# A float32 decoder trunk: the second MLP product as seven half-sized products, with the residual stream kept as [token, feature]

## The chip, the cores and the metric

The kernel runs on one core of a Trainium2 chip. The metric is the device time of one execution in microseconds (us), as the median of several runs. The engines are named as in the profile: PE (TensorE: matmuls and transposes, with its loads of the stationary operand as PEld), DVE (VectorE), ACT (ScalarE), POOL (GpSimd), and SP (SyncE, which issues DMAs).

## The reference

A trunk of two layers over 512 tokens of 1024 features in float32: layer 0 mixes tokens by stick-breaking attention, layer 1 by a gated linear recurrence (HGRN2), and an MLP follows each. Before each part stands an RMSNorm, behind it an addition to the residual stream.

```python
def squared_relu_mlp(h, w1, w2):          # w1: 1024 x 4096, w2: 4096 x 1024
    a = jax.nn.relu(h @ w1)
    return (a * a) @ w2

for layer in range(2):
    h = rmsnorm(x, norm_gains[layer, 0])
    x = x + (stick_breaking_mixer(h, ...) if layer == 0 else hgrn2_mixer(h, ...))
    h = rmsnorm(x, norm_gains[layer, 1])
    x = x + squared_relu_mlp(h, mlp_w1[layer], mlp_w2[layer])
```

## The kernel before

Every large product is computed in three passes: each operand is split into a rounded part `hi` (type fp32r) and the rest `lo`, and `hi*hi + hi*lo + lo*hi` is summed in PSUM. A matmul takes a stationary block of 128x128 and a moving operand of up to 512 columns, so one output tile over 1024 inputs takes 8 x 3 = 24 matmuls.

The residual stream is kept transposed: eight tiles `xT` of [128 features, 512 tokens] (L347). In `gemm_w` (L314) weights are stationary and 512 tokens move past them. A weight slab is 1024 rows by 256 columns. `Weights.prepare` (L274) loads it in two halves (`wr`, three buffers), ACT casts each half to `wh` (L265), DVE subtracts to get `wl` (L266); `wh` and `wl` have two buffers each. `Weights.next` hands out one slab and prepares the following, so a slab is prepared while its predecessor is used, and cannot be before the one ahead of that is done with.

`mlp` (L656) runs four rounds over blocks of 1024 hidden features. A round takes four slabs of w1 and makes eight hidden tiles: DVE evacuates PSUM with relu and the norm's factor into `u` (L674), ACT squares it (`a`, L678), DVE splits it into `hh` and `hl` (L680, L681). Then four slabs of w2 make eight output tiles, which DVE adds to `xT` (L697). PSUM tiles of the tag `mm` have two buffers, `z` two, `tr` three.

A norm's inputs are split from `xT` tile by tile as they are completed (`Norm.add`, L366); the sums of squares over features are made by ACT squares, DVE additions and small matmuls (`sums`, L376). `finish` (L393) computes r = 1/rms and spreads it over the partitions as `R` while `two` (L649) already multiplies the first slab. At the end `store` (L980) transposes each output tile back on PE, ACT copies it to SBUF and SP sends it out.

PE's order is the order of the program, with side tasks (`Line`, L120) placed by waits in `LAG` counted in estimated PE time. The order on the other engines is made by the scheduler of the framework when the kernel is built, by the program's order and its own estimates; on the chip every engine then takes its queue strictly in that order.

Of the kernel before, what the change touches and what calls it, by code (L numbers as in the profile page):

```python
# [30 lines left out]
def level_columns(H, skip):  # L31
# [8 lines left out]
    "st": 4.96,  # L40
    "bc": 4.0,
# [8 lines left out]
    "o": 2.04,  # L50
# [8 lines left out]
def trunk(  # L59
# [209 lines left out]

    class Weights:  # L270
# [3 lines left out]
        def prepare(self):  # L274
            if self.plan:
                hi, lo, load, split = slab_halves(self.plan.pop(0))
                for a in range(2):
                    split(a, load(a))
                self.ready.append((hi, lo))
# [67 lines left out]
    xT = [cp.tile([P, S], F32, name=f"xT{k}") for k in range(KT)]  # L347

    class Norm:


        def __init__(self, layer, j):
            self.layer, self.j = layer, j
            self.acts, self.acc = [], None

        def split(self, k, src=None):
            src = xT[k] if src is None else src
# [6 lines left out]
            self.acts.append((hi, lo))  # L364

        def add(self, k):  # L366
            self.split(k)
            if self.acc is None:
                self.acc = sb("bc", name="acc")
                nc.scalar.activation(out=self.acc, in_=xT[k], func=AF.Square)  # L370
            else:
                sq = sb("sq", name="sq")
                nc.scalar.activation(out=sq, in_=xT[k], func=AF.Square)
                nc.vector.tensor_add(self.acc, self.acc, sq)

        def sums(self):  # L376
            p = ps("tr", name="ps_st")
            for t in range(TT):
                mm(p[:, t : t + 1], blk(self.acc, t), ones[:, 0:1], True, True)
            return p[:, 0:TT]  # L380
# [12 lines left out]
        def finish(self):  # L393

            yield LAG["st"]
            sums = self.sums()
            _, self.r = self.stats(sums)
# [20 lines left out]
    def attention(norm):  # L418
# [23 lines left out]
        ss = sb("ss", (P, 4, TT), name="ssx")  # L442
        wsl, xin, raws = start["w"], start["x"], start["raws"]
        first = [ps("mm"), ps("mm"), ps("z"), ps("z")]
        with tc.manual_schedule(
            engines={mybir.EngineType.Activation, mybir.EngineType.DVE}
        ):
            for c in range(5):
                if c < 4:
                    turned = []  # L450
                    for j in range(2):
                        k = 2 * c + j
                        p = ps("tr", name="ps_x")
                        for t in range(TT):
                            tr(blk(p, t), xin[c][:, t, j * P : (j + 1) * P])
                        norm.split(k, p)
                        turned.append(p)
# [630 lines left out]
```

## Time and profile before

| | |
|---|---|
| median of 3 runs | 1311.36 us (1311.09 to 1312.01) |
| the profiled execution | 1314.0 us, span 1312.3 us |
| granted PE clock, mean | 0.997 |
| PE / DVE / ACT / POOL busy | 98% / 61% / 34% / 6% |
| attention and its projection | 0 to about 309 us |
| first MLP | about 309 to 659 us |
| recurrence and its projection | about 659 to 955 us |
| second MLP | about 955 us to the end |
| weights and inputs read | 107.4 MB, mean 83 GB/s over the span with the output |

In rows of groups of instructions the columns are: line, engine, operation, output<-inputs by the program's names, shape, count; then busy us and mean ns of one; then the idle time of the engine just before them and what ended it. A row of the timeline gives start, length, engine, line, operation, operands and count, and in brackets the idle time before it. In a row of one tile's instructions three numbers stand for the shortest, the median and the longest, in ns. Matmuls are pipelined: a matmul that is listed with 389 ns is followed by the next after less than that.

### The profile page before, as it was taken

To read this page: it belongs to the slowest core of one execution; us is meant where nothing else is said; L and a number is where in the kernel's file an instruction comes from. 1 tells how busy PE (TensorE), PEld (TensorE's weight loads), DVE (VectorE), ACT (ScalarE), POOL (GpSimd) and SP (SyncE) were. 2 spreads that over 40 slices of the span, in tenths; PEclk is the share of its full clock that TensorE was granted. 3 is DMA by queue.
4 is the path that set the end of the run, shared out by engine and by line. 5 is a ranking of instruction groups with operands and counts; after the bars stand their busy time and mean duration, and the time that the engine had idled before them with its cause. 6 is when DMAs were issued, how large, how long until landed. Compare 5 with 4: busy or idle time off the path is not lost.

```text
span 1312.3 us, 17619 instructions
## 1 busy us (share of the span) xinstructions
PE 1288.4 (98%) x6993; PEld 1103.6 (84%) x6993; DVE 798.1 (61%) x1534; ACT 446.0 (34%) x756; POOL 79.7 (6%) x139
## 2 busy tenths in 40 slices
PE   7999999999999999999999999999999999999998
PEld 7989898778888888888888888888888888888887
DVE  5787688768534435345578888787774354453441
ACT  5555454544212222123433333342432122221221
POOL 0100000000000000000013222222000000000000
PEclk9999999999999999999999999999999999999999
DMA  6312121113333333333321312221323333333331
GB/s 181 107 33 65 33 65 65 45 52 94 97 98 97 97 96 98 96 96 97 97 85 47 94 58 72 65 65 65 96 86 103 95 99 98 95 100 95 99 96 48
DMA packets 110658, 110.64 MB, mean 84 GB/s; under 512 B 3849, under 2 KB 106417, under 8 KB 110577
## 3 DMA queue, kind: packets, MB, share of 16 engines
q1 hardware_dynamic: 110496, 109.22, 26.9%
q8 instruction: 55, 0.90, 0.3%
q0 software_dynamic: 80, 0.31, 0.1%
q14 instruction: 27, 0.21, 0.1%
HBM read 107.41 MB, written 2.10 MB: 83 GB/s over the span
## 4 chain that ended last, share of the span: by engine, by line
PE 83%; DVE 10%; issue 2%; POOL 2%; ACT 1%; SPq 1%; DMA 0%; DVEq 0%; POOLq 0%; ACTq 0%
PE ps_mm L153 70%; PE po L153 3%; PE ps_z L153 3%; POOL tot L814 2%; DVE sc L847 2%; DVE wl L266 2%; PE ps_s L153 2%; PE pa L157 1%; PE z L153 1%; DVE qr L828 1%; PE po_h L153 1%; DVE sn L593 1%; DVE X L865 1%; DVE X L869 1%; DVE ql L565 1%
## 5 line engine op out<-in xcount | busy, mean ns | idle before, releaser
L265 ACT CAST wh<-wr 128x1024 fp32r<-128x1024 f32 x198 | 199.9, 1052 | 391.2 <-PE ps_mm L153 355.5
L266 DVE TENSOR_TENSOR wl<-wr,wh 128x1024 fp32r<-128x1024 f32 x198 | 237.4, 1229 | 17.5 <-ACT wh L265 16.8
L153 PE MATMUL ps_mm<-xh,wh 128*128 128x512 f32 x592 | 232.1, 392 | 0.0
L153 PE MATMUL ps_mm<-xh,wl 128*128 128x512 f32 x592 | 230.5, 389 | 0.0
L153 PE MATMUL ps_mm<-xl,wh 128*128 128x512 f32 x592 | 230.4, 389 | 0.0
L153 PE MATMUL ps_mm<-hh,wh 128*128 128x512 f32 (+1 forms) x520 | 201.3, 387 | 0.0
L153 PE MATMUL ps_mm<-hh,wl 128*128 128x512 f32 (+1 forms) x520 | 200.7, 386 | 0.0
L153 PE MATMUL ps_mm<-hl,wh 128*128 128x512 f32 (+1 forms) x520 | 200.6, 386 | 0.0
L153 PE MATMUL ps_mm<-wh,xh 128*128 128x256 f32 x592 | 173.3, 293 | 0.0
L153 PE MATMUL ps_mm<-wl,xh 128*128 128x256 f32 x592 | 167.7, 283 | 3.8 <-DVE wl L461 3.3
L153 PE MATMUL ps_mm<-wh,xl 128*128 128x256 f32 x592 | 167.5, 283 | 0.0
L697 DVE TENSOR_TENSOR xT<-xT,ps_mm 128x512 f32<-128x512 f32 x63 | 43.3, 687 | 203.5 <-PE ps_mm L153 203.5
L153 PEld LDWEIGHTS ps_mm<-xh,wl 128*128 128x128 f32 x592 | 111.1, 188 | 23.1
L153 PEld LDWEIGHTS ps_mm<-xl,wh 128*128 128x128 f32 x592 | 111.2, 188 | 22.6
L153 PEld LDWEIGHTS ps_mm<-xh,wh 128*128 128x128 f32 x592 | 111.2, 188 | 22.5
L153 PEld LDWEIGHTS ps_mm<-wl,xh 128*128 128x128 f32 x592 | 113.4, 192 | 4.8 <-DVE wl L461 3.5
L153 PEld LDWEIGHTS ps_mm<-wh,xh 128*128 128x128 f32 x592 | 113.2, 191 | 4.2 <-issue 3.6
L674 DVE SCALAR_TENSOR_TENSOR u<-ps_mm,R 128x512 f32<-128x512 f32 x60 | 41.5, 691 | 123.1 <-PE ps_mm L153 123.1
L153 PEld LDWEIGHTS ps_mm<-hl,wh 128*128 128x128 f32 x520 | 97.7, 188 | 19.6
L153 PEld LDWEIGHTS ps_mm<-hh,wl 128*128 128x128 f32 x520 | 97.7, 188 | 19.6
L153 PEld LDWEIGHTS ps_mm<-hh,wh 128*128 128x128 f32 x520 | 97.7, 188 | 19.5
L153 PEld LDWEIGHTS ps_mm<-wh,xl 128*128 128x128 f32 x592 | 113.4, 192 | 0.0
(213 smaller groups left out, 1651.6 us busy)
## 6 DMA issues: line engine op xcount, KB each, us to landing
wr<-in_mlp_w_dram SPq DMA_DIRECT2D x128, 512.0 KB, 3.8
wr<-in_hg_w_in_dram SPq DMA_DIRECT2D x32, 512.0 KB, 3.8
wr<-in_sb_w_qkv_dram SPq DMA_DIRECT2D x22, 512.0 KB, 3.6
wr<-in_sb_w_o_dram SPq DMA_DIRECT2D x8, 512.0 KB, 4.3
wr<-in_hg_w_o_dram SPq DMA_DIRECT2D x8, 512.0 KB, 3.6
xin<-in_x_dram SPq DMA_DIRECT2D x8, 256.0 KB, 5.4
out_dram<-o SPq DMA_DIRECT2D x7, 256.0 KB, 2.3
wr<-in_sb_w_qkv_dram SPq DMA_DIRECT2D x4, 256.0 KB, 5.4
```

The costliest lines, as they stand in the source:

```text
L153: nc.tensor.matmul(o, lhsT=lhsT, rhs=rhs, start=start, stop=stop, **kw)
L157: nc.tensor.transpose(o, in_, ident)
L265: nc.scalar.copy(hi[:, c, :], raw)
L266: nc.vector.tensor_tensor(out=lo[:, c, :], in0=raw, in1=f(hi[:, c, :]), op=ALU.subtract)
L565: nc.vector.tensor_tensor(out=ql[i][own, :], in0=pq[own, :], in1=f(qh[i][own, :]), op=ALU.subtract)
L593: nc.vector.tensor_tensor_scan(out=rev, data0=rev, data1=later[:, S - W :][:, ::-1], initial=1.0, op0=ALU.mult, op1=ALU.max,)
L674: nc.vector.scalar_tensor_tensor(out=u, in0=p, scalar=0.0, in1=norm.R, op0=ALU.max, op1=ALU.mult)
L697: nc.vector.tensor_add(xT[m], xT[m], p)
L814: nc.gpsimd.tensor_tensor(out=tots[H][:, :, None], in0=t0, in1=t1, op=ALU.mult)
L828: nc.vector.tensor_tensor(out=q1, in0=q1, in1=t0.to_broadcast([P, S // (2 * H), H]), op=ALU.mult)
L847: nc.vector.copy_predicated(out=o, mask=mask.rearrange("p (g w) -> p g w", g=g)[:, None].to_broadcast([P, 2, g, w]), data=data.rearrange(" ...
L865: nc.vector.tensor_tensor(out=o, in0=qv[:, :, :, part * H : part * H + w], in1=tv[:, :, :, part - 1, None].to_broadcast([P, TT, g, w]), op ...
```

## The change

The second product of a round is h (512 tokens x 1024) times a 1024x1024 block of w2. Both are cut into quarters: A11, A21 (tokens 0-255 and 256-511 of hidden tiles 0-3), A12, A22 (of tiles 4-7), and B11, B12, B21, B22. Seven products of quarter size replace eight (Winograd's form of Strassen's identity). They use A11, A12, A22 and four sums of quarters (`s1` to `s4`), and B11, B21, B22 and four differences. The results go back into the residual stream by additions, some through a tile `U`.

- *Stationary and moving.* The output is now [token, feature]: activation blocks are stationary, 512 columns of weights move (`chain`). The residual stream is two tiles `xt[h]` of [128, 4 token tiles, 512 features]. The output projections of the mixers use the same form.
- *Activations* (`Seven.take`). Tiles 0-3: ACT squares and casts, DVE subtracts for A11, POOL makes the difference A11-A21. Tiles 4-7: ACT squares and casts three times, DVE makes three `lo` of 512 columns (`a2l`, `s31l`, `s42l`) and two subtractions of 256 columns (`a`), POOL one addition of 256.
- *Weights* (`quarters`, `seven`). The four quarters of a w2 block are loaded whole during the w1 slabs into tiles of other tags (B, X5, R4). Seven slabs of 512 rows by 512 columns are split from them; the `lo` of two are made on POOL, of five on DVE. Of the four differences, POOL makes three (called T1, T3 and the last) and DVE one (T2), each in two subtractions of 1024 columns.
- *Norms.* Squares are summed by ACT with an accumulator (`squares`). Both halves of the features are turned by PE transposes (`turning`) and split from PSUM; `two` multiplies the half that is ready first. The initial copies into `xT` go, and the output is sent straight from `xt`.

```diff
+        def slab(src, eng=nc.vector):
...
+            for a in range(2):
+                c = slice(2 * a, 2 * a + 2)
+                nc.scalar.copy(hi[:, c, :], src[a])
+                eng.tensor_tensor(out=lo[:, c, :], in0=src[a], in1=f(hi[:, c, :]), op=ALU.subtract)
+            return hi, lo
+        def b11():
+            got = slab(b[0, 0])
+            minus(nc.gpsimd, b[0, 0], b[0, 1], b[0, 0])
+            minus(nc.gpsimd, b[0, 1], b[1, 1], b[0, 1])
+            return got
+        def t1():
+            got = slab(b[0, 0])
+            minus(nc.vector, b[0, 0], b[1, 1], b[0, 0])
+            return got
+        def t2():
+            got = slab(b[0, 0])
+            minus(nc.gpsimd, b[1, 0], b[1, 0], b[0, 0])
+            return got
+        slabs = [
+            b11, lambda: slab(b[1, 0], nc.gpsimd), t1, t2, lambda: slab(b[1, 1], nc.gpsimd),
+            lambda: slab(b[0, 1]), lambda: slab(b[1, 0]),
+        ]
...
-            got += [full(mlp_w1[layer], 0, q * D + c * SLAB) for c in range(4)]
-            got += [full(mlp_w2[layer], q * D, c * SLAB) for c in range(4)]
+            loads, slabs = seven(mlp_w2[layer], q * D)
+            for c in range(4):
+                got += [full(mlp_w1[layer], 0, q * D + c * SLAB), loads[c]]
+            got += slabs
...
+        def turning(self, h, lag):
+            yield lag
+            for k in range(4 * h, 4 * h + 4):
+                p = ps("tr", name="ps_x")
+                for t in range(TT):
+                    tr(blk(p, t), blk(xt[h][:, t, :], k - 4 * h))
+                self.split(k, p)
+                yield LAG["x2"]
...
+    def chain(o, wsl, acts):
+        hi, lo = wsl
+        n = len(acts)
+        for k, (ah, al) in enumerate(acts):
+            mm(o, ah, hi[:, k, :], k == 0, False)
+            mm(o, ah, lo[:, k, :], False, False)
+            mm(o, al, hi[:, k, :], False, k == n - 1)
+            yield
...
+            k -= 4
+            a, raw = sb("sn", name="a"), self.raw[k]
+            self.raw.append(a)
+            nc.scalar.activation(out=a, in_=u, func=AF.Square)
+            nc.gpsimd.tensor_tensor(out=raw[:, B], in0=raw[:, B], in1=a[:, B], op=ALU.add)
+            self.a2.append(self.two_parts(a, "Q", "a2"))
+            nc.vector.tensor_tensor(out=a[:, B], in0=a[:, B], in1=raw[:, A], op=ALU.subtract)
+            nc.vector.tensor_tensor(out=a[:, A], in0=a[:, A], in1=a[:, B], op=ALU.subtract)
+            self.s31.append(self.two_parts(raw, "qT", "s31"))
+            self.s42.append(self.two_parts(a, "Q" if k < 2 else "qT", "s42"))
...
+        steps = [
+            ("a11", p1), ("a12", p2), ("s1", p5), ("s2", p6), ("s4", p3), ("s3", p7), ("a22", p4),
+        ]
+        for n, (name, then) in enumerate(steps):
+            wsl = weights.next()
+            for t in range(2):
+                p = ps("z" if n % 2 else "mm", name="ps_mm")
+                yield from chain(p, wsl, A.part(name, t))
+                then(t, p)
```

In `LAG`, "st" (4.96) and "o" (2.04) go, "x" 1.6, "x7" 3.0 and "x2" 0.5 come, and "bc" goes from 4.0 to 8.5.

The change also reorders what stands in the queues. On DVE, before, around the last two hidden tiles of the first MLP's second round (numbers are those of the program's tiles; `u_4291` and `u_4324` are the tiles 6 and 7):

```order
L674 SCALAR_TENSOR_TENSOR u_4291<-ps_mm_4266,R_3534 128x512 [waits PE_49]
L680 CAST hh_4295<-a_4293 128x512 [waits Activation_49]
L681 TENSOR_TENSOR hl_4296<-a_4293,hh_4295 128x512 [waits DVE_49]
L674 SCALAR_TENSOR_TENSOR u_4324<-ps_mm_4299,R_3534 128x512 [waits PE_49]
L266 TENSOR_TENSOR wl_4333<-wr_4334,wh_4332 128x1024 [waits DMAHW1_49,Activation_49]
L266 TENSOR_TENSOR wl_4333<-wr_4338,wh_4332 128x1024 [waits DMAHW2_49,Activation_49]
L680 CAST hh_4328<-a_4326 128x512 [waits Activation_49]
L681 TENSOR_TENSOR hl_4329<-a_4326,hh_4328 128x512 [waits DVE_49]
L697 TENSOR_TENSOR xT0_99<-xT0_99,ps_mm_4342 128x512 [waits PE_49]
```

Now, in the same place, from tile 5's `a2l` to tile 7's evacuation (`a_4340` belongs to tile 5, `u_4396` and `a_4398` to tile 6, `u_4440` to tile 7):

```order
L780 TENSOR_TENSOR a2l_4344<-a_4340,a2h_4343 128x512 [waits Activation_49]
L772 TENSOR_TENSOR a_4340<-a_4340,raw_a_4169 128x256 [waits DVE_49,Pool_49]
L780 TENSOR_TENSOR s31l_4350<-raw_a_4169,s31h_4349 128x512 [waits Activation_49]
L773 TENSOR_TENSOR a_4340<-a_4340 128x256 [waits DVE_49]
L854 SCALAR_TENSOR_TENSOR u_4396<-ps_mm_4371,R_3520 128x512 [waits PE_49]
L780 TENSOR_TENSOR s42l_4354<-a_4340,s42h_4353 128x512 [waits Activation_49]
L780 TENSOR_TENSOR a2l_4402<-a_4398,a2h_4401 128x512 [waits Activation_49]
L780 TENSOR_TENSOR s31l_4408<-raw_a_4216,s31h_4407 128x512 [waits Activation_49]
L772 TENSOR_TENSOR a_4398<-a_4398,raw_a_4216 128x256 [waits DVE_49]
L773 TENSOR_TENSOR a_4398<-a_4398 128x256 [waits DVE_49]
L780 TENSOR_TENSOR s42l_4412<-a_4398,s42h_4411 128x512 [waits Activation_49]
L854 SCALAR_TENSOR_TENSOR u_4440<-ps_mm_4415,R_3520 128x512 [waits PE_49]
```

Between two evacuations of PSUM there stood two instructions on a tile; now there stand six, some of which wait for POOL (by themselves, or by ACT's cast of what POOL made).

On POOL, before, nothing stood between the attention's clearing of `ql` and the recurrence:

```order
L559 MEMSET ql_2767 64x512
L559 MEMSET ql_2768 64x512
L559 MEMSET ql_2847 64x512
L559 MEMSET ql_2848 64x512
L814 TENSOR_TENSOR tot_5914<-fr_5885 128x256
L814 TENSOR_TENSOR tot_5914<-tot_5914 128x128
```

Now, in the same round as above, with `raw_4095`/`raw_4097` the two halves of B11, `raw_4175`/`raw_4177` of B12, `raw_4255`/`raw_4257` of B22, `raw_4357`/`raw_4359` of B21, and the 256-column additions those of tiles 4 to 7:

```order
L770 TENSOR_TENSOR raw_a_4136<-raw_a_4136,a_4296 128x256 [waits Activation_49,Pool_49]
L293 TENSOR_TENSOR raw_4095<-raw_4175,raw_4095 128x1024 [waits DMAHW4_49,DMAHW2_49,DVE_49]
L770 TENSOR_TENSOR raw_a_4169<-raw_a_4169,a_4340 128x256 [waits Activation_49,Pool_49]
L293 TENSOR_TENSOR raw_4175<-raw_4255,raw_4175 128x1024 [waits DMAHW6_49,Pool_49]
L293 TENSOR_TENSOR raw_4097<-raw_4177,raw_4097 128x1024 [waits DMAHW5_49,DMAHW3_49,DVE_49]
L293 TENSOR_TENSOR raw_4177<-raw_4257,raw_4177 128x1024 [waits DMAHW7_49,Pool_49]
L770 TENSOR_TENSOR raw_a_4216<-raw_a_4216,a_4398 128x256 [waits Activation_49]
L305 TENSOR_TENSOR wl_4460<-raw_4357,wh_4459 128x1024 [waits DMAHW0_49,PE_49,Activation_49]
L305 TENSOR_TENSOR wl_4460<-raw_4359,wh_4459 128x1024 [waits DMAHW1_49,Activation_49]
L770 TENSOR_TENSOR raw_a_4249<-raw_a_4249,a_4442 128x256 [waits Activation_49]
L293 TENSOR_TENSOR raw_4357<-raw_4357,raw_4095 128x1024 [waits DVE_49,Pool_49]
L293 TENSOR_TENSOR raw_4359<-raw_4359,raw_4097 128x1024 [waits DVE_49,Pool_49]
```

The four subtractions for T1 and T3 stand ahead of the addition for tile 6, and the two `lo` of the second slab ahead of that for tile 7.

More of the change, by code (lines that the diff above doesn't have):

```diff
@@ L49 @@
     "m": 8.82,
-    "o": 2.04,
     "head": [
@@ L353, in __init__, with split @@
             self.layer, self.j = layer, j
-            self.acts, self.acc = [], None
-        def split(self, k, src=None):
-            src = xT[k] if src is None else src
+            self.acts, self.ss, self.turned = [None] * KT, None, []
+        def split(self, k, src):
             g = gain(self.layer, self.j, k)
@@ L664, in mlp @@
                 if q + c == 0:
-                    early = yield from two(wsl, norm.acts)
+                    early = yield from two(wsl, norm)
                     yield [task]
@@ L713, in hgrn @@
             if hp == 0:
-                early = yield from two(wsl, acts)
+                early = yield from two(wsl, norm)
                 yield [task]
@@ L998, in trunk_steps @@
         nxt = Norm(1, 0)
-        yield from mlp(norm, nxt.add)
+        yield from mlp(norm, nxt)
         line.width = 3
```

248 lines of the change are left out of this document (153 added, 95 removed).

## The prediction

> **What bounds the kernel now.** I read the head of the page, then PE's own waits, then one window of 100 us inside the second MLP.
>
> ```profile
> span 1312.3 us, 17619 instructions
> ...
> PE 1288.4 (98%) x6993; PEld 1103.6 (84%) x6993; DVE 798.1 (61%) x1534; ACT 446.0 (34%) x756; POOL 79.7 (6%) x139
> ```
> ```profile
> PE ps_s L153 <- DVE sc L847: 6.6, 16, 0.7
> PE ps_mm L153 <- DVE wl L461: 3.3, 1, 3.3
> ...
> PE ps_mm L153 <- DVE wl L266: 0.5, 1, 0.5
> ```
> ```profile
> 1000.00:1100.00 100.00, 100.00 (x443) 82.81 (x442) 45.18 (x57) 24.83 (x29) 0.00 (x0) 1.00 0.31 95
> ```
>
> The columns of the last row are PE, PEld, DVE, ACT and POOL busy, then the granted clock. In the MLP PE never pauses, and in the whole run it waited 0.5 us for a weight slab (L266). 100 us hold 443 matmuls of 512 columns, so one costs 0.2257 us. DVE is under half busy and POOL does nothing there. The MLP's time is its number of matmuls, as long as the others keep up: a matmul removed is gained, a wait of PE is lost in full.
>
> **What PE loses and gains.** A round has 8 outputs of 24 matmuls in the second product, 192; afterwards 7 products of 24, 168. Eight rounds lose 192 matmuls: 192 x 0.2257 = -43.3 us. Which operand is stationary changes nothing in that pitch, since each matmul has its own load either way. Each of the three later norms now needs 32 transposes, and the 32 of the output go: 64 more. The sums over partitions go.
>
> ```profile
> 1293.29 0.60 PE L157 MATMUL ps_o<-ident,xT 128*128 128x128 f32 x4
> ```
> ```profile
> 960.84 0.95 PE L153 MATMUL ps_st<-ones,acc 128*128 128x1 f32 x8
> 961.65 0.47 PE L153 MATMUL ps_z<-xh,wh 128*128 128x512 f32 x1
> ```
> ```profile
> L692 DVE TENSOR_TENSOR xT<-xT,ps_mm 128x256 f32<-128x256 f32 x2 | 0.8, 420 | 5.1 <-PE ps_mm L153 5.1
> L465 DVE COPY xT<-ps_x 128x512 f32<-128x512 f32 x4 | 2.7, 683 | 0.0
> ```
> ```profile
> L464 ACT COPY xT<-ps_x 128x512 f32<-128x512 f32 x4 | 2.4, 589 | 3.2 <-DVE xl L361 3.2
> ```
> ```profile
> 1308.69 0.41 PE L157 MATMUL ps_o<-ident,xT 128*128 128x128 f32 x2 [0.39 <-DVE xT L692]
> ...
> 1309.18 0.37 ACT L986 COPY o<-ps_o 128x256 f32<-128x256 f32 x1 [0.42 <-PE ps_o L157]
> ```
>
> Four transposes span 0.60 us and one lasts 0.27 (0.41 for two, 0.60 for four: 0.1 apart), so the pitch is 0.109 and 64 add 7.0. The sums took 961.65 - 960.84 = 0.81 a norm, three times: -2.4. At the end the last transposes and the copy (0.8) give way to an addition of 512 columns for 256 (0.69 below for 0.42): -0.5. At the start four copies on each of DVE and ACT go, and PE waited 3.3 us for DVE there; I take -1.0 between nothing and all of DVE's 2.7. Together -40.2: from the median 1311.4 to 1271.2. (The profiled execution took 1314.0, span 1312.3 and 1.7 around it, 2.6 above the median; its durations are used, the sum is made from the median.)
>
> **What the others now do.** Prices:
>
> ```profile
> L266 DVE TENSOR_TENSOR wl<-wr,wh 128x1024 fp32r<-128x1024 f32 x198 | 237.4, 1229 | 17.5 <-ACT wh L265 16.8
> L681 DVE TENSOR_TENSOR hl<-a,hh 128x512 fp32r<-128x512 f32 x64 | 44.3, 693 | 2.2
> L674 DVE SCALAR_TENSOR_TENSOR u<-ps_mm,R 128x512 f32<-128x512 f32 x60 | 41.5, 691 | 123.1 <-PE ps_mm L153 123.1
> ```
> ```profile
> L265 ACT CAST wh<-wr 128x1024 fp32r<-128x1024 f32 x198 | 199.9, 1052 | 391.2 <-PE ps_mm L153 355.5 <-PE ps_z L153 26.0 <-issue 3.3
> L678 ACT ACTIVATE a<-u 128x512 f32<-128x512 f32 x64 | 40.3, 631 | 120.0 <-DVE u L674 120.0
> ```
> ```profile
> L820 POOL TENSOR_TENSOR kk<-kk,tot x48: 615/749/1659, 692.8 to 906.0; 128x256 f32<-128x256 f32 x48
> ```
> ```profile
> L814 POOL TENSOR_TENSOR tot<-tot x40: 216/342/642, 679.3 to 877.8; 128x128 f32<-128x128 f32 x8, 128x64 f32<-128x64 f32 x8, 128x32 f32<-128x32 f32 x8, 128x16 f32<-128x16 f32 x8
> ```
>
> A slab now serves 24 matmuls (5.42 us), not 48 (10.83). Its two casts on ACT (2.0) and two subtractions on DVE (2.4) still fit. POOL gets ten 1024-column subtractions a round. No row has one; call its price p. The quickest 256-column one took 0.615 and the quickest narrow one (8 or 16) 0.216: 1.66 ns a column, so 0.22 + 1008 x 0.00166 = 1.9 as an estimate. Four times 0.615, 2.46, is the dear end, DVE's 1.23 for the same shape the cheap one. I take 1.9, being worked out from rows of the same operation.
>
> By the Trainium skill ("GPSIMD Engine Reference", section "Performance versus the Vector engine") a 2048-column fp32 addition took 4497 ns there; half is 2.25 us, an estimate, by which the sum below would end at 1357. No run here shows a wide one.
>
> **POOL and DVE get in each other's way.** The rows of the recurrence show it:
>
> ```profile
> 697.73 1.50 POOL L820 TENSOR_TENSOR kk<-kk,tot 128x256 f32<-128x256 f32 x2 [3.33 <-PE ps_s L153]
> ```
> ```profile
> 698.33 0.50 DVE L847 COPY_PREDICATED sc<-masks,ps_s 128x32 f32<-128x32 uint8 x2
> 698.70 1.60 DVE L266 TENSOR_TENSOR wl<-wr,wh 128x1024 fp32r<-128x1024 f32 x1
> ```
> ```profile
> 702.54 1.79 POOL L820 TENSOR_TENSOR kk<-kk,tot 128x256 f32<-128x256 f32 x2 [3.32 <-PE ps_s L153]
> ```
> ```profile
> 701.76 1.23 DVE L266 TENSOR_TENSOR wl<-wr,wh 128x1024 fp32r<-128x1024 f32 x1
> 702.91 0.93 DVE L865 TENSOR_TENSOR X<-qr,tot 128x128 f32<-128x128 f32 x2
> ```
> ```profile
> 741.21 0.85 POOL L814 TENSOR_TENSOR tot<-fr 128x256 f32<-128x256 f32 x1 [22.34 <-DVE fr L737]
> 742.14 1.07 POOL L814 TENSOR_TENSOR tot<-tot 128x128 f32<-128x128 f32 x2
> ```
> ```profile
> 742.09 0.43 DVE L883 TENSOR_TENSOR qr<-qr,tot 128x256 f32<-128x256 f32 x1 [0.50 <-POOL tot L814]
> ```
>
> wl, whose two inputs lie in SBUF, began at 698.70 while POOL worked until 699.23, and took 1.60 for 1.23: it stood until 0.16 us before POOL's end. From 701.76 it is POOL that stands (1.79 for two), and then the two X, between POOL's two. The predicated copies, fed from PSUM, ran through POOL's work. So such pairs exclude each other and take turns, handing over some 0.15 us before an end; a DVE instruction that waits for POOL starts 0.03 after it (742.06 to 742.09), POOL's next 0.08, so DVE then goes first. Evacuations of PSUM are free of it.
>
> The Trainium skill ("SBUF — State Buffer", section "Who interferes with whom") has the same lock, but held for the whole instruction. The trace is milder by 0.15 a hand-over; ten of them a round would make 12 us more, 1347.
>
> **Where PE will wait.** Time 0 is the first matmul of a round's last w1 slab; k=5's output is in PSUM then, k=6's at 5.4, k=7's at 10.8. DVE finishes k=4, evacuates u5 (to 1.0) and makes the two lows of slab B11 (to 3.65). POOL's first subtraction has waited since 2.5. Now turns are taken in the order of the two queues: POOL 1024 to 3.5+p, a2l to 4.1+p, POOL's 256 to 4.6+p, a[B] to 5.1+p, POOL 1024 to 4.95+2p, s31l to 5.5+2p, POOL 1024 to 5.4+3p, a[A] to 5.7+3p, and only then u6, to 6.3+3p (12.0 at p=1.9). The first chain of product 1 takes u6's PSUM buffer and wants it at 10.83. The second wants u7's at 13.54. In DVE's queue u7 stands behind all of k=6: POOL's fourth 1024 (5.6+4p), s42l of k=5 (6.1), POOL's addition for k=6, which is queued behind those four (6.65), s31h on ACT (7.3), s31l (8.0), two 256-column ones (8.8), s42h on ACT (9.4), s42l (10.1), u7 (10.7+4p). PE waits (10.7+4p) - 13.5 = 4p-2.8 in product 1.
>
> Next, the two lows of the second slab end on POOL at 10.5+6p, which product 2 just bears. Slab 4 is the next late one: POOL's addition for k=7, ACT's cast, two lows of slab 3, two additions, T2's two subtractions and POOL's 1024 between them bring its first low to 20.1+7p, and PE wants it at 24.5+4p (two products after u7): 3p-4.4. Its second low comes after another POOL 1024 and two additions, p-0.4 late. With 0.4 for s42l of k=7 behind it product 4 waits 4p-4.4. Products 5 to 7 have slack.
>
> A round waits 8p-7.2: 2.6 us at 1.23, 8.0 at 1.9, 12.5 at 2.46. Eight rounds: 21, 64, 100. The sum is 1271.2 + 64 = 1335; break-even (40.2/8 = 5.0 a round) lies at p=1.53.
>
> **Edits costed at nothing.**
>
> ```profile
> wr<-in_mlp_w_dram SPq DMA_DIRECT2D x128, 512.0 KB, 3.8
> ```
>
> The quarters of w2 are as many bytes in as many transfers; the last is issued at time 0 and used after 14, against 3.8; gone, that cover costs the rest of the transfer. SP's queue behind it holds the next round's w1, a stage early. At a norm, half of the first slab's matmuls (24, 5.4 us) run while the other half's features are turned and split; without that cover each of three norms costs about 2 us, so +-3 in all. The broadcast of r waits 8.5 us of PE work, under those 48 matmuls. The swapped operands of the projection cost the same matmuls.
>
> **Rivals.** (1) *POOL is cheap*: a dense 1024 costs below 1.53, down to 1.23, since the rows behind p are broadcast or strided reads. Then the round waits 2.6 to 5.0: 1292 to 1309. For it: nothing dense was measured; against: 1.66 ns a column on every width seen. This is the other side, and decides at p=1.53. 0.24. (2) *PE is covered*: the takes finish in time in spite of the order, PE waits under 1.5 us a round: 1271 to 1283. Against it, u7 stands behind POOL's four subtractions even if nothing is blocked (p=1.23 leaves 2.1). 0.10. (3) *POOL is dear*, 2.2 to 2.46: 1354 to 1371, or two instructions of POOL in a row keep DVE out. 0.12; the skill's price above is of this kind. (4) The two effects cancel within 0.2% (2.6 us, about what a measurement of this kernel can tell from no change): 0.07.
>
> **How the numbers follow.** The forecast, p of 1.6 to 2.2 and 1316 to 1354 around 1335, has 0.47. Faster is rivals 1 and 2, 0.34; the same 0.07; slower 0.59. From the cheap end of p less the norms' 3 us, but without rival 2, to the foot of rival 3: 1285 to 1360, which leaves out rival 2 and most of rival 3.
>
> **What would show it.** PE's matmul rows fall by 192 and its pitch stays 0.226. PE's waits gain two groups of 8 (or 16): the first product's ps_mm on DVE u, 4 to 5 us a round, and the fourth's on DVE wl, about 3. POOL's 1024-column mean, blocked time aside, is 1.9; DVE's subtractions from SBUF lengthen beside it and its evacuations from PSUM don't. I am wrong if PE's busy share in the MLP stays at 100%, if POOL's price is under 1.5, or if the waits stand at the norms.

## The result, and the profile after

The changed kernel takes 1420.0 us (median of 4 runs, 1418.3 to 1421.2), the kernel before, run beside it, 1311.4. The ratio is 1.083 (95% interval 1.081 to 1.084): slower, as forecast, but by 109 us and not by 24, and outside the range.

The head of the page of the changed kernel, with the row of the granted clock:

```profile
span 1416.5 us, 17879 instructions
...
PE 1303.9 (92%) x6817; PEld 1088.8 (77%) x6817; DVE 1007.0 (71%) x1671; ACT 566.1 (40%) x943; POOL 419.8 (30%) x331
...
PEclk9999999999899999999999999999998998999998
```

The window of one round of the first MLP, from the last matmul of one w1 stage to the same matmul a round later (PE, PEld, DVE, ACT and POOL busy, granted clock, DMA share, GB/s):

```profile
454.29:553.33 99.04, 88.00 (x361) 69.76 (x360) 66.93 (x69) 36.47 (x48) 42.64 (x25) 0.95 0.26 85
```

A round has 360 matmuls, 81.25 us at the old pitch of 0.2257. It lasts 99.04, so 17.8 us are lost in it. Before, a round had 384 matmuls and lasted 86.7 us; it is 12.4 longer now, and eight times that is 99 of the 109 us. Two things are seen here. PE is idle for a part of the round, and the clock is 0.95, where it was 1.00 in the window of before.

PE's waits over the whole run (us in total, times, longest), and the timeline of PE at the round's first pause and in its fourth product:

```profile
PE ps_mm L154 <- ACT s42h L779: 35.5, 8, 4.4
PE ps_mm L154 <- DVE wl L305: 26.9, 16, 1.8
PE ps_mm L154 <- DVE s42l L780: 10.9, 8, 1.6
PE ps_mm L154 <- DVE xt L702: 6.9, 7, 1.0
```
```profile
454.29 0.39 PE L154 MATMUL ps_mm<-xh,wl 128*128 128x512 f32 x1
459.12 0.77 PE L154 MATMUL ps_mm<-wh,a 128*128 128x512 f32 x1 [4.44 <-ACT s42h L779]
459.69 0.63 PE L154 MATMUL ps_mm<-wl,a 128*128 128x512 f32 x1
460.12 0.63 PE L154 MATMUL ps_mm<-wh,a 128*128 128x512 f32 x1
...
481.34 0.51 PE L154 MATMUL ps_mm<-wl,s42h 128*128 128x512 f32 x1 [1.78 <-DVE wl L305]
484.68 0.51 PE L154 MATMUL ps_mm<-wl,s42h 128*128 128x512 f32 x1 [1.67 <-DVE wl L305]
487.46 0.50 PE L154 MATMUL ps_mm<-wh,s42l 128*128 128x512 f32 x1 [1.58 <-DVE s42l L780]
```

The long pauses stand where the prediction put them: ahead of product 1 and in product 4, at both lows of its slab and at `s42l`. The releaser that is named for the first one misleads. The product's operands (`a`, tiles 0 to 3) had long been there; the evacuation `u` of tile 6, whose PSUM buffer the product takes, ended at 458.98, 0.14 before PE went on. Behind the pause the matmuls follow each other after 0.43 us in place of 0.23 (459.69 to 460.12): that is the clock. These are the 3.41 us behind the first pause and behind the last (granted clock 0.50 and 0.57):

```profile
459.12:462.53 3.41, 3.40 (x8) 2.73 (x9) 2.69 (x5) 1.76 (x3) 0.73 (x1) 0.50 0.00 0
487.46:490.87 3.41, 3.41 (x9) 2.69 (x10) 0.69 (x1) 0.00 (x0) 3.41 (x2) 0.57 0.55 174
```

What happened on POOL and on DVE in that first pause:

```profile
446.01 3.32 POOL L293 TENSOR_TENSOR raw<-raw 128x1024 f32<-128x1024 f32 x1 [5.37 <-DVE wl L305]
449.29 1.19 POOL L770 TENSOR_TENSOR raw_a<-raw_a,a 128x256 f32<-128x256 f32 x1
450.43 7.67 POOL L293 TENSOR_TENSOR raw<-raw 128x1024 f32<-128x1024 f32 x3
```
```profile
446.98 2.89 DVE L780 TENSOR_TENSOR a2l<-a,a2h 128x512 fp32r<-128x512 f32 x1
450.50 2.60 DVE L772 TENSOR_TENSOR a<-a,raw_a 128x256 f32<-128x256 f32 x1 [0.63 <-POOL raw_a L770]
453.03 2.87 DVE L780 TENSOR_TENSOR s31l<-raw_a,s31h 128x512 fp32r<-128x512 f32 x1
455.82 2.56 DVE L773 TENSOR_TENSOR a<-a 128x256 f32<-128x256 f32 x1
458.30 0.68 DVE L854 SCALAR_TENSOR_TENSOR u<-ps_mm,R 128x512 f32<-128x512 f32 x1
```

Four instructions of 0.4 to 0.7 us take 2.6 to 2.9 each, one beside each of POOL's four subtractions, and the evacuation stands behind them. The tile view gives POOL's price (shortest, median and longest, in ns):

```profile
L305 DVE TENSOR_TENSOR wl<-raw,wh x80: 1211/1219/2223, 345.7 to 1403.9; 128x1024 fp32r<-128x1024 f32 x80
...
L293 POOL TENSOR_TENSOR raw<-raw x48: 2389/2616/3317, 347.0 to 1383.0; 128x1024 f32<-128x1024 f32 x48
L305 POOL TENSOR_TENSOR wl<-raw,wh x32: 2387/2842/3354, 365.3 to 1389.5; 128x1024 fp32r<-128x1024 f32 x32
...
L293 DVE TENSOR_TENSOR raw<-raw x16: 1216/2166/3122, 376.3 to 1379.8; 128x1024 f32<-128x1024 f32 x16
```

Alone, 1024 columns take 2.39 us on POOL and 1.22 on DVE; beside each other POOL's take up to 0.96 us more (3.354) and DVE's up to 1.9 (3.122). The evacuations of PSUM did not lengthen, as the row by form shows (mean 688 ns, 691 before):

```profile
L854 DVE SCALAR_TENSOR_TENSOR u<-ps_mm,R 128x512 f32<-128x512 f32 x60 | 41.3, 688 | 90.7 <-PE ps_mm L154 90.7
```

The theory to be tested: PE waits because POOL's 1024-column instructions, by their length and by shutting DVE out, delay what stands behind them in DVE's queue; and each long pause costs again, because the clock is lower after it. The rivals: the choice of PSUM buffers, the layout with its norms, too much work on DVE whoever shares it, the number of activation sums.

### The profile page after: what moved, and what is told of

It is laid out like the page before. It is cut to its first block, busy times and chain, and to the rows that moved or that the text cites. A ratio compares the mean times of both kernels' runs of the same rounds, so it can differ in the third digit from the quotient of the medians.

```text
span 1416.5 us, 17879 instructions
## 1 busy us (share of the span) xinstructions
PE 1303.9 (92%) x6817; PEld 1088.8 (77%) x6817; DVE 1007.0 (71%) x1671; ACT 566.1 (40%) x943; POOL 419.8 (30%) x331
## 5 line engine op out<-in xcount | busy, mean ns | idle before, releaser
L267 DVE TENSOR_TENSOR wl<-wr,wh 128x1024 fp32r<-128x1024 f32 x134 | 177.9, 1346 | 14.2 <-ACT wh L266 13.7
L266 ACT CAST wh<-wr 128x1024 fp32r<-128x1024 f32 x134 | 136.4, 1052 | 122.9 <-PE ps_mm L154 117.8
L304 ACT CAST wh<-raw 128x1024 fp32r<-128x1024 f32 x112 | 112.0, 1047 | 141.3 <-PE ps_mm L154 120.5
L293 POOL TENSOR_TENSOR raw<-raw 128x1024 f32<-128x1024 f32 x48 | 132.4, 2766 | 105.0 <-DVE raw L293 61.5
L764 POOL TENSOR_TENSOR raw_a<-raw_a 128x256 f32<-128x256 f32 x32 | 23.6, 739 | 352.6 <-DVE a L763 237.1
L305 DVE TENSOR_TENSOR wl<-raw,wh 128x1024 fp32r<-128x1024 f32 x80 | 109.6, 1402 | 6.5 <-ACT wh L304 6.5
L702 DVE TENSOR_TENSOR xt<-xt,ps_mm 128x512 f32<-128x512 f32 x128 | 85.1, 678 | 34.6 <-PE ps_mm L154 34.4
L305 POOL TENSOR_TENSOR wl<-raw,wh 128x1024 fp32r<-128x1024 f32 x32 | 90.7, 2855 | 30.8 <-ACT wh L304 30.8
L154 PE MATMUL ps_mm<-wh,a 128*128 128x512 f32 x128 | 56.3, 507 | 38.9 <-ACT s42h L779 35.5
```

The costliest lines, as they stand in the source:

```text
L154: nc.tensor.matmul(o, lhsT=lhsT, rhs=rhs, start=start, stop=stop, **kw)
L266: nc.scalar.copy(hi[:, c, :], raw)
L267: nc.vector.tensor_tensor(out=lo[:, c, :], in0=raw, in1=f(hi[:, c, :]), op=ALU.subtract)
L293: eng.tensor_tensor(out=o[a], in0=x[a], in1=y[a], op=ALU.subtract)
L304: nc.scalar.copy(hi[:, c, :], src[a])
L305: eng.tensor_tensor(out=lo[:, c, :], in0=src[a], in1=f(hi[:, c, :]), op=ALU.subtract)
```

## The experiments

### z_first: product 1 takes other PSUM buffers

```diff
-                p = ps("z" if n % 2 else "mm", name="ps_mm")
+                p = ps("mm" if n % 2 else "z", name="ps_mm")
```

> Only the PSUM buffers of the products change places: products 1, 3, 5 and 7 take the two buffers of the tag z, products 2, 4 and 6 those of mm, so that product 1 no longer takes the buffer of the hidden tiles 6 and 7. Theory A (the queue of DVE, held up by POOL's subtractions of 2.39 us, decides; slab 4's first low comes 37.6 us after the start of the last w1 slab whatever PE does before): the 4.6 us pause ahead of product 1 goes, and about as much comes back ahead of products 2 and 4; 1390 to 1420 us. Theory B (the choice of the buffer is the cause): 8 times the pause of 4.6 us and the slower matmuls behind it are gained, 1350 to 1385 us.

Measured: 1410.4 us (ratio to before 1.074, 1.071 to 1.077), in theory A's range and far from B's. Product 1 starts without a pause, and the pause comes one product later (PE's timeline):

```profile
460.57 0.39 PE L154 MATMUL ps_mm<-wh,a 128*128 128x512 f32 x1
465.19 0.80 PE L154 MATMUL ps_mm<-wh,a2h 128*128 128x512 f32 x1 [4.22 <-ACT wh L304]
467.62 0.80 PE L154 MATMUL ps_mm<-wl,a2h 128*128 128x512 f32 x1 [1.64 <-POOL wl L305]
```

The buffer is not the cause. What is late is the queue: whatever PE does first, it meets much the same lateness in the next thing that it needs. The 10 us that the run does gain are not taken apart here.

### dve_all: POOL's work given to DVE

```diff
-            minus(nc.gpsimd, b[0, 0], b[0, 1], b[0, 0])
+            minus(nc.vector, b[0, 0], b[0, 1], b[0, 0])
...
-            b11, lambda: slab(b[1, 0], nc.gpsimd), t1, t2, lambda: slab(b[1, 1], nc.gpsimd),
+            b11, lambda: slab(b[1, 0]), t1, t2, lambda: slab(b[1, 1]),
...
-            nc.gpsimd.tensor_tensor(out=raw[:, B], in0=raw[:, B], in1=a[:, B], op=ALU.add)
+            nc.vector.tensor_tensor(out=raw[:, B], in0=raw[:, B], in1=a[:, B], op=ALU.add)
```

> Every sum and difference of the seven products that POOL made (per round ten of 1024 columns, eight of 256, six of 512) is made by DVE. Theory A (a pair of POOL and DVE instructions from SBUF exclude each other, so that POOL's 2.39 us for 1024 columns cost DVE more than the 1.23 us of doing them itself): PE's waits fall from about 12 to 4 to 7 us a round; 1305 to 1340 us, DVE about 90% busy inside the MLP. Theory C (DVE's queue has too much in it, whoever does the 1024s): DVE gets about 20 us more a round, the evacuations stand further back; no gain, 1400 us and more.

Measured: 1363.7 us (1.039, 1.037 to 1.041): 56 us less than the changed kernel, though DVE has more to do. That is theory A's direction and not theory C's, but above A's range. PE has one pause a round left (waits of PE, then DVE's timeline at it):

```profile
PE ps_mm L154 <- DVE wl L305: 61.2, 8, 7.7
```
```profile
367.38 3.49 DVE L293 TENSOR_TENSOR raw<-raw 128x1024 f32<-128x1024 f32 x3
370.78 0.69 DVE L780 TENSOR_TENSOR s42l<-a,s42h 128x512 fp32r<-128x512 f32 x1
371.38 1.22 DVE L305 TENSOR_TENSOR wl<-raw,wh 128x1024 fp32r<-128x1024 f32 x1
```

PE resumes at 372.66 with the second half of slab 2 (the eighth matmul of product 2, not the second as the expectation says). Its low stands behind three differences that are needed only later. So the order in the queue may be a second cause, beside POOL; dve_even and the runs after it test that.

### bare and layout: what is left without the sums

`bare` leaves out all sums and differences of quarters, in `take` and in the slabs; `layout` computes eight plain products in the new layout.

```diff
-            minus(nc.gpsimd, b[0, 0], b[0, 1], b[0, 0])
-            minus(nc.gpsimd, b[0, 1], b[1, 1], b[0, 1])
...
+            a = sb("sn", name="a")
+            nc.scalar.activation(out=a, in_=u, func=AF.Square)
+            self.a2.append(self.two_parts(a, "Q", "a2"))
```

> All sums and differences of quarters are left out: the hidden tiles are squared, cast and split alone, the seven slabs are split from the plain quarters, and all of it on DVE; the seven products, their evacuations, the additions to the residual stream, the layout and the norms stay. So part of the computation is missing. Theory A (the work of the sums on DVE and POOL is the whole loss): PE's sum of 1271 us, 1268 to 1280. Theory D (a part of the loss lies in the swapped operands, the evacuations or the norms): above 1290 us.

```diff
-            loads, slabs = seven(mlp_w2[layer], q * D)
...
+            got += [half(mlp_w2[layer], q * D + r, c) for r in (0, D // 2) for c in (0, D // 2)]
...
+        for part in range(2):
+            for h in range(2):
+                wsl = weights.next()
+                for t in range(TT):
+                    p = ps("mm")
+                    acts = [[blk(a, t) for a in pair] for pair in A.a2[4 * part : 4 * part + 4]]
+                    yield from chain(p, wsl, acts)
+                    back(h, t, p)
...
```

> Eight plain products in place of the seven: the residual stream stays [token, feature], activation tiles stay stationary, the second product is four slabs of 512 rows by 512 columns with four chains of 12 matmuls each, and no sums or differences. Theory A: the layout alone costs the 64 transposes and saves the sums, the last copy and the copies at the start: 1311.4 + 7.0 - 2.4 - 0.5 - 1.0 = 1314.5 us, 1310 to 1319. Theory D (the layout with its norms or stationary activations costs much by itself): above 1330 us.

Measured: bare 1281.9 us (0.977, 0.976 to 0.979), layout 1318.0 (1.005, 1.003 to 1.006), each beside 1311.8. Bare lies just above theory A's 1280, well below D's 1290. Bare saves 29.9 us and not 40.2. The layout costs 6.2 and not 3.1, and from layout to bare the seven products save 36.1 and not 43.3. A part of the missing ten shows in bare at the norm ahead of the recurrence, where PE waits for the splits of the turned features:

```profile
641.73 0.66 PE L158 MATMUL ps_x<-ident,xt 128*128 128x128 f32 x4 [2.37 <-DVE xl L427]
644.85 0.66 PE L158 MATMUL ps_x<-ident,xt 128*128 128x128 f32 x4 [0.64 <-DVE xl L427]
646.79 0.66 PE L158 MATMUL ps_x<-ident,xt 128*128 128x128 f32 x4 [0.58 <-DVE xl L427]
652.87 0.47 PE L154 MATMUL ps_bc<-dg,ones_r 128*128 128x512 f32 x1 [0.87 <-DVE dg L485]
```

That is 4.5 us. No other norm shows such a wait: the ones ahead of the two MLPs have one of 0.22 us each.

### no_diff: the weight differences left out

```diff
-            minus(nc.gpsimd, b[0, 0], b[0, 1], b[0, 0])
-            minus(nc.gpsimd, b[0, 1], b[1, 1], b[0, 1])
...
-            minus(nc.vector, b[0, 0], b[1, 1], b[0, 0])
...
-            minus(nc.gpsimd, b[1, 0], b[1, 0], b[0, 0])
```

> The four differences of weight quarters are left out (per round six subtractions of 1024 columns on POOL, two on DVE); the sums of the activations, the two slabs whose lows POOL makes, and all else stay as in the changed kernel. So part of the computation is missing. Theory A (POOL's 1024-column subtractions between DVE's activation sums are what PE waits for; without them DVE's queue gets to hidden tiles 6 and 7 in time): the pauses ahead of products 1 and 4 go, 1282 to 1300 us against 1281.9 without any sums. Theory E (the activation sums, with six DVE instructions between two evacuations, are the greater part): above 1340 us.

Measured: 1292.6 us (0.986, 0.985 to 0.988), in theory A's range. All activation sums are still made, four lows a round are still made on POOL, and this is the largest group of PE's waits that is left:

```profile
PE ps_mm L154 <- DVE xt L698: 6.9, 7, 1.0
```
So of the 138 us between bare and the changed kernel, 127 hang on eight subtractions of 1024 columns a round, six of them on POOL. Which part is POOL's and which the place in the queue, this run does not tell.

### dve_warm: spare matmuls in the pause

```diff
+            if fill and k == 0:
+                d = ps("av", name="ps_d")
+                for _ in range(fill):
+                    mm(d, ah, hi[:, k, :], True, True)
...
+                yield from chain(p, wsl, A.part(name, t), 32 if (n, t) == (1, 0) else 0)
```

> The kernel with all sums on DVE (1363.7 us, one pause of 7.8 us a round at product 2's second matmul, then 8 matmuls at 0.43 us in place of 0.23), and 32 more matmuls of 512 columns into a spare PSUM buffer, never read, put into that pause: 7.2 us of work for a pause of 7.8. Theory F (the lower clock after a pause costs PE time that nothing hides): the clock stays at 1 in every round and 8 x (8 x 0.2) = 13 us are gained, 1346 to 1354 us. Theory G (DVE is late in that stretch anyway, a slower PE only waits less afterwards): within 4 us of 1363.7.

Measured: 1346.2 us (1.027, 1.025 to 1.028) against the 1363.7 of dve_all: 17.5 us less, with 256 matmuls more, and inside theory F's range. Both rows of the clock are from windows of 3.4 and 16 us behind the same place, without and with the spare matmuls:

```profile
372.66:376.07 3.41, 3.41 (x8) 2.73 (x9) 2.90 (x3) 0.00 (x0) 0.00 (x0) 0.50 0.00 0
```
```profile
364.00:380.00 16.00, 15.59 (x68) 12.46 (x67) 13.23 (x16) 2.85 (x3) 0.00 (x0) 1.00 0.17 56
```

The slow stretch behind the pause is a loss of its own, 2.2 us a round here (17.5/8). Theory G falls for this kernel.

### dve_even and dve_order: less in DVE's queue just ahead of the products

In `dve_even` the halves are the even and the odd hidden tiles:

```diff
-                r = r0 + i * (D // 2) + a * 2 * P
+                r = r0 + a * 4 * P
...
-                    out=t, in_=w[r : r + 2 * P, j * S : (j + 1) * S].rearrange("(k p) c -> p k c", p=P)
+                    in_=w[r : r + 4 * P, j * S : (j + 1) * S].rearrange("(k i p) c -> i p k c", i=2, p=P)[i],
...
-            if k < 4:
+            if k % 2 == 0:
...
```

> All sums on DVE, and the halves of the hidden tiles are the even and the odd ones instead of the first and the last four (the quarters of w2 take rows to match), so that the heavy hidden tiles (4.05 us on DVE each against 1.55) are spread over the four slabs of w1 and no longer stand together ahead of the products. Theory A (what counts is what stands in DVE's queue just ahead of the products: 2 of 4 heavy tiles go from there): 1300 to 1330 us against 1363.7. Theory H (DVE's total, some 74 of 81 us a round, is the bound, where it stands is no matter): within 10 us of 1363.7.

In `dve_order` the differences are built up the other way round:

```diff
-            minus(nc.vector, b[0, 0], b[0, 1], b[0, 0])
-            minus(nc.vector, b[0, 1], b[1, 1], b[0, 1])
+                nc.vector.tensor_tensor(out=b[0, 0][a], in0=b[0, 1][a], in1=b[0, 0][a], op=ALU.add)
...
+        def t3():
+            minus(nc.vector, b[0, 1], b[1, 1], b[0, 1])
...
-            ("a11", p1), ("a12", p2), ("s1", p5), ("s2", p6), ("s4", p3), ("s3", p7), ("a22", p4),
+            ("a11", p1), ("a12", p2), ("s2", p6), ("s1", p5), ("s4", p3), ("s3", p7), ("a22", p4),
```

> The same, and the differences are made in another order that needs no more storage: B22-B12 first, as soon as the two are loaded (during the w1 slabs), then + B11 once that slab is split, then B21 and B22 minus that; products 3 and 4 change places to match. As many operations as before. Theory A: only two 1024-column operations are left in the last w1 slab in place of four, and two move to where DVE has slack; PE's waits fall to 1 to 3 us a round, 1284 to 1310 us, faster than the kernel before. Theory H (DVE's total is the bound): no gain over the run with even and odd tiles.

Measured: 1331.1 us (1.015, 1.013 to 1.017), at the upper end of theory A's range, and 1328.6 (1.013, 1.011 to 1.014), well outside it. The first move gains 33 us with the same instructions, so their place counts; the second gains next to nothing, as theory H had it. But H's reason does not hold, for PE's waits show one place again, and the next experiment removes it:

```profile
PE ps_mm L154 <- DVE s42l L785: 24.0, 8, 3.1
```

### even_late and even_late_pool: the order mended, and POOL put back

`even_late` moves three things: product B22 comes third, hidden tile 7's parts get priority over the differences, and B22-B12 is tied to a hidden tile by a factor that is 1.

```diff
-            ("a11", p1), ("a12", p2), ("s2", p6), ("s1", p5), ("s4", p3), ("s3", p7), ("a22", p4),
+            ("a11", p1), ("a12", p2), ("s4", p3), ("s2", p6), ("s3", p7), ("s1", p5), ("a22", p4),
...
-                    A.take(u)
+                    with tc.high_priority(offset=400 if (c, j) == (3, 1) else 0):
+                        A.take(u)
...
-            minus(nc.vector, b[0, 1], b[1, 1], b[0, 1])
+                nc.vector.scalar_tensor_tensor(
+                    out=b[0, 1][a], in0=b[1, 1][a], scalar=weights.one, in1=b[0, 1][a],
+                    op0=ALU.mult, op1=ALU.subtract,
+                )
```

> All sums on DVE, even and odd halves, and three moves in the queues on top of the last run (1328.6 us, where one pause of 3.45 us a round was left, at product 3's s42l, which stood behind four differences): the product with B22 comes third, so that the four differences after B21 have one product more of time; hidden tile 7's parts are given priority over them; B22-B12 is tied to hidden tile 2 of the same round, so that it stands in the second w1 slab, where DVE has 2.7 us to spare. As many operations as before. Theory A (only what stands ahead of what in DVE's queue decides, DVE's total of some 74 of 81 us fits): PE waits 1 to 2 us a round, 1286 to 1305 us, faster than the kernel before by 0.5 to 2%. Theory H (DVE's total is the bound): 1320 to 1330 us.

`even_late_pool` gives six of the sums and differences back to POOL:

```diff
-                nc.vector.tensor_tensor(out=b[0, 0][a], in0=b[0, 1][a], in1=b[0, 0][a], op=ALU.add)
+                nc.gpsimd.tensor_tensor(out=b[0, 0][a], in0=b[0, 1][a], in1=b[0, 0][a], op=ALU.add)
...
-            minus(nc.vector, b[1, 0], b[1, 0], b[0, 0])
-            minus(nc.vector, b[0, 0], b[1, 1], b[0, 0])
+            minus(nc.gpsimd, b[1, 0], b[1, 0], b[0, 0])
+            minus(nc.gpsimd, b[0, 0], b[1, 1], b[0, 0])
```

> The same kernel with six of its eight 1024-column sums and differences a round given to POOL (the two for T2, the two for T4, the two for T1); all else the same. DVE has 7.3 us a round less to do, POOL 14.3 more. Theory A (while POOL reads from SBUF, DVE's subtractions from SBUF stand; 2.39 us of POOL cost DVE more than the 1.22 of doing it): slower than the same kernel with all on DVE by 3 to 8 us a round, 24 to 64 us. Theory I (in a good order POOL is a relief for DVE): no slower, or faster.

Measured: even_late 1282.8 us (0.978, 0.976 to 0.980), faster than both kernels, below theory A's range, and as fast as bare, which makes no sums at all. A round is the 81.25 us of its matmuls, with PE never idle (the window of one round; granted clock 1.00):

```profile
1000.00:1081.25 81.25, 81.25 (x358) 66.94 (x357) 67.55 (x92) 35.84 (x47) 0.00 (x0) 1.00 0.32 104
```

even_late_pool takes 1313.0 us (1.001, 1.000 to 1.002): six operations a round on POOL cost 30 us, 3.8 a round, inside theory A's 3 to 8. First all on DVE, the head of the page and one group:

```profile
PE 1255.6 (98%) x6817; PEld 1070.6 (83%) x6817; DVE 1021.6 (80%) x1871; ACT 566.8 (44%) x943; POOL 79.6 (6%) x139
```
```profile
L793 DVE TENSOR_TENSOR a2l<-a,a2h 128x512 fp32r<-128x512 f32 x32 | 21.9, 683 | 0.0
```

Then with POOL, the same head and group, and PE's largest wait in the MLP:

```profile
PE 1265.5 (96%) x6817; PEld 1071.5 (82%) x6817; DVE 1057.3 (81%) x1823; ACT 566.2 (43%) x943; POOL 216.3 (16%) x187
```
```profile
L793 DVE TENSOR_TENSOR a2l<-a,a2h 128x512 fp32r<-128x512 f32 x32 | 57.0, 1780 | 0.0
```
```profile
PE ps_mm L154 <- DVE a2l L793: 15.3, 8, 1.9
```

Two of the four `a2l` of a round, those of tiles 5 and 7, now take 2.9 us (the mean of all is 1780 ns for 683), and PE waits for the second of them. The scheduler also put some of DVE's instructions elsewhere in the queue; in even_late no `a2l` takes more than 0.69 us, wherever it stands. DVE got rid of 48 operations of 1.22 us, 58 us, and is busy for 36 us more than with them. So each operation on POOL held DVE up for (58 + 36)/48 = 1.96 us, an estimate from the busy times of two profiled executions, where doing it costs DVE 1.22.

### after_warm and pauses: the clock by itself

`after_warm` puts spare matmuls into the pauses of the changed kernel, `pauses` puts pauses into the kernel before.

```diff
+                fill = {0: {("ahead", 0): 20}, 3: {("lo", 0): 8, ("lo", 2): 8, ("al", 3): 6}}
```

> The changed kernel, with spare matmuls of 512 columns into a PSUM buffer that is never read, put where PE pauses in every round: 20 ahead of product 1 (4.5 us of its pause of 4.6), 8, 8 and 6 at the three pauses in product 4 (about 1.8, 1.8 and 1.4 us). Theory G1 (the slower matmuls of product 1 cost nothing, since slab 4's low comes at its own time; those behind product 4 cost 1.7 to 3.4 us a round): 14 to 27 us less, 1393 to 1407. Theory F1 (every slow matmul is lost, 5 us a round): 40 us less, 1380 and below. Theory K (the clock doesn't matter here): 1416 to 1424.

```diff
+            d = sb("AT", dt=F32R, name="d")
+            nc.vector.tensor_copy(d, u)
+            for _ in range(2 * (4 * norm.layer + q)):
+                nc.vector.tensor_tensor(
+                    out=d[:, : 2 * P], in0=f(d[:, : 2 * P]), in1=f(d[:, 2 * P :]), op=ALU.max
+                )
+            mm(ps("av", name="ps_d"), d[:, :P], d, True, True)
```

> The kernel before, with one pause of PE ahead of the second product of each of the eight rounds: a spare matmul waits for a chain on DVE that starts with hidden tile 7 and has 0, 2, 4 ... 14 more steps of 0.43 us, so pauses of about 1 to 8 us. Theory F (a pause by itself lowers the clock for a while afterwards, from some length on): behind the longer pauses matmuls follow each other every 0.43 us for 3.4 us or a multiple, behind the shorter ones every 0.23; 1311 + 36 for the pauses + 1.7 for each drop: 1350 to 1365 us. Theory L (the clock falls for another reason, such as the mix of work in the products): no drop in any of the eight rounds, 1340 to 1352 us.

Measured: after_warm 1426.7 us (1.086, 1.084 to 1.088), no faster than the changed kernel (1.083) and above all three ranges. The spare matmuls filled the first pause, and the second chain of product 1, now at full clock, ran into the wait for tile 7's evacuation, which the slow clock had hidden:

```profile
458.79 4.70 PE L154 MATMUL ps_d<-wh,a 128*128 128x512 f32 x20
...
466.01 0.39 PE L154 MATMUL ps_mm<-wh,a 128*128 128x512 f32 x1
469.00 0.79 PE L154 MATMUL ps_mm<-wh,a 128*128 128x512 f32 x1 [2.61 <-DVE u L864]
```

So in product 1 of the changed kernel the slow clock cost little, as theory G1 said: DVE's queue ends the wait either way, for tile 7's evacuation ends 10.3 us after the start of the last w1 matmul without the spare matmuls and 10.4 with them. The gain that G1 saw behind product 4 did not come. In its place stand new pauses (this one is 21.0 us in eight times) and 9.5 us of spare matmuls a round (42 x 0.2257). What the clock alone costs the changed kernel is not settled by this run.

pauses takes 1383.7 us (1.053, 1.051 to 1.056). The pauses came out longer than planned (1.7 to 10.9 us from start to start), which puts the time above both ranges. The rows behind the shortest and the next, and the granted clock in 3.4 us behind each:

```profile
352.15 0.47 PE L153 MATMUL ps_d<-d 128*128 128x512 f32 x1 [1.34 <-DVE d L684]
352.46 0.40 PE L153 MATMUL ps_mm<-hh,wh 128*128 128x512 f32 x1
...
443.15 0.76 PE L153 MATMUL ps_d<-d 128*128 128x512 f32 x1 [3.48 <-DVE d L686]
443.72 0.63 PE L153 MATMUL ps_mm<-hh,wh 128*128 128x512 f32 x1
```
```profile
352.15:355.55 3.40, 3.40 (x15) 2.83 (x16) 3.15 (x4) 1.00 (x2) 0.00 (x0) 1.00 0.35 119
443.16:446.57 3.41, 3.41 (x8) 2.73 (x9) 1.59 (x2) 0.00 (x0) 0.00 (x0) 0.50 0.65 183
```

Seven of the eight pauses, all but the shortest, were followed by 7 to 12 matmuls at 0.43 us. A pause alone does it, in a kernel that has no such drop in its MLP otherwise.

## Why the prediction was wrong

The direction and the mechanism were right: DVE and POOL shut each other out from SBUF, evacuations of PSUM stay free of it, the waits stand ahead of product 1 and in product 4, and the change loses. Its size was too small by 85 us. By the prediction's own steps:

- *The price p* failed first. 1.9 us was taken, 2.39 measured. The price of a column was too low: 1.66 ns, from a row of 0.615 us at 256 columns with one operand that is broadcast. POOL's plain instructions here took 0.73 us at 256 columns and 2.39 at 1024, which works out to 2.16 ns a column on a fixed part of about 0.18 us, near the 0.22 that was taken. By the text's own formula, 8p - 7.2 is 11.9 us a round at 2.39, not 8.0, so p alone is 31 us in all. The Trainium skill's price ("GPSIMD Engine Reference", section "Performance versus the Vector engine"), halved to 2.25 as an estimate, was nearer than the text's value, and still below the trace.
- *The order of the turns* failed in one place. The text let DVE go first at each handover, so that tile 6's evacuation stood behind three of POOL's subtractions and ended at 6.3 + 3p, 13.5 us after the start of the last w1 slab (443.64) at 2.39. In the trace POOL's second subtraction started at 450.43 and DVE's `a` at 450.50, all four stood ahead of that evacuation, and it ended 15.3 after. The pause ahead of product 1 was 4.6 us, not 2.6. Later points came out nearer: tile 7's evacuation ended 21.0 after, for 10.7 + 4p = 20.3, and slab 4's first low let PE go on 37.7 after (481.34), for 20.1 + 7p = 36.8.
- *The sum of the pauses* is nearly right at the measured price, partly by luck. The pauses of the round at 454 us, from start to start less the pitch, sum to 12.2. Of this, 5.1 stand in product 1 (the formula: 6.8; the slow matmuls of its first chain lost 2.4 us, which the second wait would otherwise have taken) and 5.5 in product 4 (the formula: 5.2). The other 1.6 the formula did not have: 0.5 at a low of product 2, and 1.15 at the start of the next round, where PE waits for an `xt` addition.
- *"Its pitch stays 0.226"* failed behind the pauses, a term that the text put at nothing without a reason. It had a wait of PE lost once, at its length. The matmuls behind a pause went at half the clock; in the round at 454 us those at 0.43 us lose another 4.6 us (from start to start less the pitch). Times eight that is 37, though some of it lies in time that PE would have waited anyway, as after_warm shows. The Trainium skill has a rule on this ("TensorE: Matmul & The Clock Gate", section "HAM oscillation — how this bites in real kernels": no idle gaps of PE over about 3.4 us). The traces agree for single pauses of 3.48 us, with a drop, and of 1.34, without. They differ for shorter ones that lowered the clock as well: seven of eight pauses of 2.6 to 3.1 us in dve_order, three of eight of 1.9 us in even_late_pool, and in seven of the changed kernel's eight rounds the three of up to 1.8 us within 8 us in product 4.
- *PE's sum* of -40.2 was -29.9 (bare). One norm of three lost its cover, 4.5 us; the text had 2 us each as the price. The layout by itself cost 3.1 more than its terms. The rest of the ten is not taken apart here.
- *Edits costed at nothing*: the quarters' transfers never end a wait of PE in the list above. PE's wait at the start of a round (6.9 us in seven times) was not among these edits.
- *The rivals.* "POOL is dear" (0.12) was the nearest, at 1354 to 1371 (1367 at 2.39), and missed for the lack of a clock term and the ten us of PE's sum. "PE is covered" and "POOL is cheap" are refuted by the pauses and by 2.39 us, "the two effects cancel" by the time.

Together: -30 for PE's work, 8 x 12.2 = 98 of pauses, 37 of slow matmuls are +105, against 109 measured. As an account of the trace this closes; as a list of what each would save it does not, since pauses and slow clock hide each other in part. no_diff and even_late show the cause without that doubt: the same products without the differences, or with all sums in a better order on DVE, show no drop of the clock in the MLP's rounds, and no pause there but the 1.0 us at the start of a round in no_diff. even_late_pool, against even_late, shows what six operations a round on POOL cost by themselves.

## What to carry to other kernels

When two engines shut each other out, as DVE and POOL did here with two operands from SBUF, giving work to the slow one need not relieve the busy one: compare what the slow engine blocks (1.96 us here) with what the fast one needs (1.22). When instructions are added to an engine that also evacuates PSUM or makes the next operand, read its queue around each hand-over to PE; as many instructions of the same sizes took 1364 us in one order and 1283 in another. And a pause of PE is priced with what follows it, so a chain of waits that looks just tolerable costs more than its length.

## What was not expected of the hardware

- After a pause the granted clock can be 0.50 for a stretch of about 3.4 us or longer, a part of which can lie in the pause, and matmuls of 512 columns then come every 0.427 us. The eight pauses of 4.44 us in the changed kernel and the seven of 3.48 us and more in pauses all brought it. Of the eight of 2.6 to 3.1 us in dve_order seven did, of the eight of 1.9 us in even_late_pool, at the same place in each round, three; single ones of 1.34 (pauses) and 2.37 us (bare) did not. What decides between those that did and those that did not is not shown.
- POOL's dense fp32 operations with two inputs took 2.39 us at 1024 columns, 1.26 at 512 and 0.73 at 256 (the quickest of each), where the rows of the recurrence, with broadcast or strided operands, had suggested 1.9 at 1024.
